# Dense experts of a diffusion step: first products of all chunks to DRAM, then the second products with three output tiles in PSUM

## The chip, the core and the metric

The kernel runs on one core of one Trainium2 chip. The metric is the device time of one launch in microseconds. Engines are named as the profile names them: PE (TensorE), DVE (VectorE), ACT (ScalarE), POOL (GpSimd), SP (SyncE, which only issues transfers here).

## The reference, cut to what matters

One layer of a diffusion backbone: modulated norm, attention and a linear recurrence, output projection, then a mixer of 16384 experts of which each token uses 16 for each of 8 heads. There are 256 context and 1024 latent tokens of 1024 features. The change is in the mixer:

```python
def peer(h, w_query, sub_keys, u_tab, v_tab):
    ...
        s1 = jnp.einsum('thq,hkq->thk', q1, sub_keys[:, 0]).astype(jnp.float32)
        s2 = jnp.einsum('thq,hkq->thk', q2, sub_keys[:, 1]).astype(jnp.float32)
        v1, i1 = lax.top_k(s1, PEER_TOPK)
        v2, i2 = lax.top_k(s2, PEER_TOPK)
        ...
        g = jax.nn.softmax(best, axis=-1)
        u = jnp.take(u_tab, eid, axis=0)
        act = jax.nn.gelu(jnp.einsum('td,thkd->thk', xb, u).astype(jnp.float32))
        vv = jnp.take(v_tab, eid, axis=0)
        return jnp.einsum('thk,thkd->td', (g * act).astype(vv.dtype), vv)
```

## The kernel before

Tokens stand in ten tiles of 128: two of context, eight latent. The mixer is computed in two ways side by side.

*Dense.* For six latent tiles (768 tokens) every expert is computed on PE, in 128 chunks of 128 experts (those that share a second key). `experts_in` (L692) makes a chunk's first products: it loads the chunk of the first table (`u`, 512 KB), splits it into two parts `uh` and `ul` that single-pass matmuls carry exactly (`split`, L132: ACT copies, another engine subtracts), and multiplies each of 8 slices of the features with the tokens' two parts `hh`, `hl`, in three matmuls (`mm3`, L137) for each of two blocks of 384 tokens: 48 matmuls of 128x384. The activations `a` are then multiplied with the routing weights `gt`, split into `ah`, `al`, and multiplied with the chunk's rows of the second table, `vh` and `vl`: six tiles, two halves of 512 features, three matmuls, so 36 matmuls of 128x512 (`dense`, L706). The results of two tiles stay in PSUM over all 128 chunks (`res`, four banks). For the other four, the products of a group of two chunks gather in a rotating bank (`rot`, two banks), which ACT copies out (`q`, L737) and DVE adds to `acc` in SBUF (L738). The first products of the first 34 chunks (`EARLY`) are taken beside the retrieval and go through DRAM (`ad`); for the others both products stand in one loop. Both splits subtract on POOL.

The weights `gt` come from DRAM too: `spread` (L644) makes, for each dense tile, one-hot matrices on DVE (`oh`), multiplies them on PE (`g`) and writes the weights of all experts to `gd`, twelve transfers of 4 MB.

*Gathered.* The two context tiles and the last two latent tiles fetch the rows of their experts: for each of 128 experts of a token one indirect transfer from POOL for each table (`mix`, L815), 512 KB into a row buffer, and one DVE operation (L829 for the first table, L843 for the second). There are 1024 of them. `tick` paces them: each piece of other work adds its estimated microseconds, and a row is issued for each `step` of them (L110). Four row buffers exist, and three more beside the dense loop (`N_MORE`).

*What sets the order.* A scheduler lays the program out once, by its own estimates, into one fixed list of instructions for each engine; an engine works through its list in order. So an instruction that waits holds up all behind it on its engine. Buffers of a pool are reused in turn, and a transfer into a buffer waits for its last reader.

The stages in the profile: modulations, context layer, latent projection, attention and norm up to 983 us; retrieval and spread of weights, with the first products of the first chunks between, to 1664 us; the dense loop with the gathered rows to the end.

## Time and profile before

| | before |
|---|---|
| median of 3 runs | 3830.61 us (3814.61 to 3831.82) |
| span of the profiled execution | 3810.7 us |
| PE busy | 3360.2 us, 88% |
| DVE busy | 3337.9 us, 88% |
| ACT busy | 1452.4 us, 38% |
| POOL busy | 2305.5 us, 61% |
| moved by DMA | 910.34 MB, 239 GB/s over the span |

The page gives the span of the profiled execution and no further time of it, so the span is compared with the runs. Two engines have the same share of the whole span, which says little: the stages differ, and a matmul's duration overlaps the next one's start. So the rows below are read by stretch, and for PE by the distance from one start to the next.

### The profile page before, as it was taken

What the parts mean: (1) busy time and instruction counts of PE and PEld (TensorE: products, weight loads), DVE (VectorE), ACT (ScalarE), POOL (GpSimd) and SP (SyncE); (2) the same over time, 40 slices, a digit from 0 to 9 for tenths busy, and PEclk for the clock granted to TensorE, in tenths of its full rate; (3) what the DMA queues carried; (4) which work ended last, traced back from release to release, by engine and by line L of the source; (5) the groups of instructions that cost most, each with busy time, mean ns of one, the idle gap of its engine ahead of it and who ended that gap; (6) DMA issues with size and microseconds to landing.
All of it is one profiled execution on the core that took longest, in us unless ns stands there. A gap on an engine that the chain in (4) does not pass through costs nothing.

```text
span 3810.7 us, 48687 instructions
## 1 busy us (share of the span) xinstructions
PE 3360.2 (88%) x16982; PEld 2714.7 (71%) x16982; DVE 3337.9 (88%) x6484; ACT 1452.4 (38%) x2270; POOL 2305.5 (61%) x1388
## 2 busy tenths in 40 slices
PE   7888869988798888878889999999999989999997
PEld 4476544433598877766667878888888878888786
DVE  4549886667889999958999999999999999999998
ACT  5634535543211345534333333333333333333333
POOL 0032664456611222136767888878888888888884
PEclk9799888999899999999999999999999999999998
DMA  8342654468810266778888888888888888888884
GB/s 331 119 148 81 216 208 140 146 214 292 278 45 23 79 193 197 209 244 305 299 298 282 287 299 288 305 294 300 298 292 292 298 302 298 292 297 296 293 302 175
DMA packets 344823, 910.34 MB, mean 239 GB/s; under 512 B 28664, under 2 KB 147064, under 8 KB 341504
## 3 DMA queue, kind: packets, MB, share of 16 engines
q0 software_dynamic: 147456, 536.94, 40.3%
q1 hardware_dynamic: 197120, 370.29, 29.3%
q8 instruction: 133, 2.18, 0.2%
q14 instruction: 114, 0.93, 0.1%
HBM read 830.55 MB, written 76.57 MB: 238 GB/s over the span
## 4 chain that ended last, share of the span: by engine, by line
DVE 29%; PE 23%; issue 10%; POOL 4%; DMA 2%; ACT 2%; SPq 0%; POOLq 0%; DVEq 0%; ACTq 0%
DVE acc L843 8%; PE u L138 5%; PE u L139 5%; PE u L140 5%; DVE row L829 4%; DVE acc L738 4%; DVE oh L676 2%; PE rot L138 2%; DVE oh L674 1%; DVE al L135 1%; DVE oh L677 1%; PE rot L140 1%; PE rot L139 1%; DVE oh L675 1%; POOL row L826 1%
## 5 line engine op out<-in xcount | busy, mean ns | idle before, releaser
L826 POOL DMA_INDIRECT row<-in_peer_u,eid x512 | 731.5, 1429 | 286.8 <-issue 81.1
L837 POOL DMA_INDIRECT row<-in_peer_v,eid x512 | 716.5, 1399 | 287.8 <-DVE acc L843 85.5
L843 DVE SCALAR_TENSOR_TENSOR acc<-row,w,acc 128x1024 f32<-128x1024 f32 x508 | 836.2, 1646 | 29.6 <-DMA row<-in_peer_v,eid 25.6
L829 DVE SCALAR_TENSOR_TENSOR row<-row,h 128x1024 f32<-128x1024 f32 x512 | 722.9, 1423 | 64.3 <-DMA row<-in_peer_u,eid 63.9
L138 PE MATMUL u<-hh,uh 128*128 128x384 f32 x2048 | 700.2, 342 | 12.7 <-ACT uh L134 9.5
L140 PE MATMUL u<-hh,ul 128*128 128x384 f32 x2048 | 698.8, 341 | 2.3 <-POOL ul L135 2.3
L139 PE MATMUL u<-hl,uh 128*128 128x384 f32 x2048 | 698.7, 341 | 0.0
L135 POOL TENSOR_TENSOR ul<-u,uh 128x1024 fp32r<-128x1024 f32 x128 | 335.4, 2635 | 369.9 <-ACT uh L134 353.9
L737 ACT ACTIVATE q<-rot 128x512 f32<-128x512 f32 x504 | 298.7, 596 | 675.6 <-DVE acc L738 373.0
L138 PE MATMUL rot<-vh,ah 128*128 128x512 f32 x1024 | 430.8, 421 | 115.7 <-ACT q L737 107.4
L738 DVE TENSOR_TENSOR acc<-q,acc 128x512 f32<-128x512 f32 x504 | 472.7, 943 | 36.2 <-ACT q L737 35.6
L139 PE MATMUL rot<-vl,ah 128*128 128x512 f32 x1024 | 411.5, 402 | 0.0
L140 PE MATMUL rot<-vh,al 128*128 128x512 f32 x1024 | 411.2, 402 | 0.0
L138 PEld LDWEIGHTS u<-hh,uh 128*128 128x128 f32 x2048 | 389.5, 190 | 18.1 <-ACT uh L134 10.4
L140 PEld LDWEIGHTS u<-hh,ul 128*128 128x128 f32 x2048 | 388.8, 190 | 3.7 <-POOL ul L135 2.7
L139 PEld LDWEIGHTS u<-hl,uh 128*128 128x128 f32 x2048 | 388.7, 190 | 2.2
L138 PEld LDWEIGHTS rot<-vh,ah 128*128 128x128 f32 x1024 | 199.5, 195 | 225.6 <-ACT q L737 188.3
L135 POOL TENSOR_TENSOR vl<-v,vh 128x1024 fp32r<-128x1024 f32 x128 | 330.5, 2584 | 27.9 <-ACT vh L134 25.9
L140 PE MATMUL mm<-hh,wl 128*128 128x256 f32 (+2 forms) x848 | 290.3, 343 | 7.4 <-POOL wl L135 5.7
L138 PE MATMUL mm<-hh,wh 128*128 128x256 f32 (+2 forms) x848 | 287.8, 339 | 5.0 <-ACT wh L134 5.0
L139 PE MATMUL mm<-hl,wh 128*128 128x256 f32 (+2 forms) x848 | 287.4, 339 | 0.0
L135 POOL TENSOR_TENSOR wl<-w,wh 128x1024 fp32r<-128x1024 f32 x46 | 113.4, 2467 | 242.4 <-ACT wh L134 242.3
(259 smaller groups left out, 6092.6 us busy)
## 6 DMA issues: line engine op xcount, KB each, us to landing
u<-in_ut SPq DMA_DIRECT2D x128, 512.0 KB, 4.3
v<-in_peer_v SPq DMA_DIRECT2D x128, 512.0 KB, 4.4
gd<-stg SPq DMA_DIRECT2D x12, 4096.0 KB, 16.4
gt<-gd SPq DMA_DIRECT2D x64, 768.0 KB, 7.6
w<-in_w_mod SPq DMA_DIRECT2D x24, 1024.0 KB, 7.6
w<-in_w_query SPq DMA_DIRECT2D x32, 512.0 KB, 3.7
w<-in_w_in SPq DMA_DIRECT2D x28, 512.0 KB, 5.0
ad<-a SPq DMA_DIRECT2D x68, 192.0 KB, 3.7
```

The lines of the kernel that those rows point to most:

```text
L135: return (eng or V).tensor_tensor(lo, src, hi, op=OP.subtract)
L138: T.matmul(out, lhs[0], rhs[0], start=first, stop=False)
L139: T.matmul(out, lhs[0], rhs[1], start=False, stop=False)
L140: T.matmul(out, lhs[1], rhs[0], start=False, stop=last)
L674: V.tensor_tensor(o1.rearrange(four, j=2), io, pairs(k1t, ts), op=OP.is_equal)
L676: V.tensor_tensor(oh.rearrange(four, j=2), o2.rearrange(four, j=2), pairs(gh, ts), op=OP.mult)
L737: A.activation(q, p, AF.Copy)
L738: tick(share / (2 * (N_DENSE - N_RES)), V.tensor_tensor(y, q, y, op=OP.add))
L826: G.indirect_dma_start(out=u, out_offset=None, in_=i["peer_u"], in_offset=bass.IndirectOffsetOnAxis(ap=eid[:, k:k + 1], axis=0))
L829: V.scalar_tensor_tensor(u, u, 1.0, h2, op0=OP.mult, op1=OP.mult, accum_out=act[:, j:j + 1])
L837: G.indirect_dma_start(out=v, out_offset=None, in_=i["peer_v"], in_offset=bass.IndirectOffsetOnAxis(ap=eid[:, k:k + 1], axis=0))
L843: V.scalar_tensor_tensor(acc, v, w[:, j:j + 1], acc, op0=OP.mult, op1=OP.add)
```

## The change

All 128 chunks' first products are computed first and written to DRAM (`ad`), beside the retrieval, the spread and a pass of their own (`phase("in")`); a second pass (`experts_out`, `phase("out")`) reads them back, chunk by chunk, with the second table and the weights. In the second pass PSUM holds three tiles (`N_RES`, six banks) and two rotating banks, in groups of four chunks; the buffers of the split tokens `hh`, `hl` are freed before it and serve the second table's splits, seven chunks deep. The subtraction of the second table's split is done by DVE, that of the first table's from chunk 60 on (`BESIDE`), and the 14 of the latent input projection. The first table's load buffer `u` is single in all first products (before: single for the early ones, double in the dense loop). The pacing constants of the gathered rows are new, and rows are now issued in the spread too.

```diff
-N_RES = 2
-GROUP = 2
-EARLY = 34
+N_RES = 3
+GROUP = 4
+AHEAD = 3
+BESIDE = 60
 F_STEP = 1.9
-D_STEP = 2.1
-STEP = {"spread": 1e9, "ret": 4.0}
-T_MUL = 2.0
-E_US = 3.0
-PE_US = 15.8
+STEP = {"spread": 3.3, "ret": 3.0, "in": 2.2, "out": 2.75}
+IN_US = 8.4
+OUT_US = 1.82
...
-            split(wh, wl, w, G if lat else V)
+            split(wh, wl, w)
...
-    ad = dram.tile([max(EARLY, 1), P, TD], F32, name="ad")
+    ad = dram.tile([P, P, TD], F32, name="ad")
...
-    def experts_in(raw, nraw, c, hh, hl, out):
-        u = raw.tile([P, KD, P], F32, name="u", bufs=nraw)
+    def experts_in(c, hh, hl):
+        u = eu.tile([P, KD, P], F32, name="u")
...
-        split(uh, ul, u, G)
+        if c < BESIDE:
+            split(uh, ul, u, G)
+        else:
+            tick(IN_US, split(uh, ul, u))
...
-            out(bs, p)
+            a = eu.tile([P, NB], F32, name="a", bufs=2)
+            A.activation(a, p, AF.Gelu_apprx_tanh)
+            nc.sync.dma_start(ad[c][:, bs], a)
...
+            NBUF = GROUP + AHEAD
+            def fetch(c):
+                v = wk.tile([P, D], F32, name="v", bufs=2)
+                nc.sync.dma_start(v, i["peer_v"].rearrange("(a b) d -> b a d", b=P)[c])
+                a = wk.tile([P, TD], F32, name="a", bufs=2)
+                nc.sync.dma_start(a, ad[c])
+                if c % 2 == 0:
+                    gts[0] = wk.tile([P, TD, 2], F32, name="gt", bufs=2)
+                    nc.sync.dma_start(gts[0], gd[c // 2])
+                vh = wk.tile([P, D], F32R, name="vh", bufs=NBUF)
+                vl = wk.tile([P, D], F32R, name="vl", bufs=NBUF)
+                tick(OUT_US, split(vh, vl, v))
+                tick(OUT_US, V.tensor_tensor(a, a, gts[0][:, :, c % 2], op=OP.mult))
+                ah = wk.tile([P, TD], F32R, name="ah", bufs=NBUF)
+                al = wk.tile([P, TD], F32R, name="al", bufs=NBUF)
+                tick(OUT_US, split(ah, al, a))
+                return c, ah, al, vh, vl
...
             for c0 in range(0, P, GROUP):
                 group = []
+                for c in range(c0, min(c0 + GROUP, P)):
+                    it = fetch(c)
+                    group.append(it)
                     if last:
-                        add(last)
+                        rotating(last)
                         last = None
+                    resident(it)
                 last = group
-            add(last)
+            rotating(last)
...
+        phase("in")
+        more.append(pool(ein, "gat2"))
+        for c in range(P):
+            experts_in(c, hha, hla)
+        more.clear()
+        behind.clear()
+    hs.close()
+    phase("out")
+    experts_out(dt)
```

How the lists of the engines change is shown at three places. In the changed kernel the lines behind the diff have moved: the gathered rows' DVE operations are L840 and L854 (L829 and L843 before), the add is L764 (L738), the multiplication with the weights L734 (L757), the gathers L837 and L848 (L826 and L837). `L135` is the subtraction of every split.

DVE in the middle of the dense loop, before:

```order
L135 TENSOR_TENSOR al<-a,ah 128x768
L843 SCALAR_TENSOR_TENSOR acc<-row,w,acc 128x1024
L757 TENSOR_TENSOR a<-a,gt 128x768
L829 SCALAR_TENSOR_TENSOR row,act<-row,h_16290 128x1024
L135 TENSOR_TENSOR al<-a,ah 128x768
L738 TENSOR_TENSOR acc_15477<-q,acc_15477 128x512
L829 SCALAR_TENSOR_TENSOR row,act<-row,h_16290 128x1024 x2
L738 TENSOR_TENSOR acc_15477<-q,acc_15477 128x512
L829 SCALAR_TENSOR_TENSOR row_21020,act<-row_21020,h_16290 128x1024
L738 TENSOR_TENSOR acc_15478<-q,acc_15478 128x512
```

DVE in the middle of the second pass, now:

```order
L764 TENSOR_TENSOR acc_22499<-q,acc_22499 128x512
L135 TENSOR_TENSOR al<-a,ah 128x768
L135 TENSOR_TENSOR vl<-v,vh 128x1024 x2
L764 TENSOR_TENSOR acc_22499<-q,acc_22499 128x512
L840 SCALAR_TENSOR_TENSOR row_27494,act<-row_27494,h_26479 128x1024
L135 TENSOR_TENSOR al<-a,ah 128x768
L844 TENSOR_TENSOR w<-w,gw_10139 128x16
L734 TENSOR_TENSOR a<-a,gt 128x768
L854 SCALAR_TENSOR_TENSOR acc<-row,w,acc 128x1024
L135 TENSOR_TENSOR vl<-v,vh 128x1024
L854 SCALAR_TENSOR_TENSOR acc<-row,w,acc 128x1024
L135 TENSOR_TENSOR al<-a,ah 128x768
```

The subtractions `vl` stand on DVE now, between fewer adds of `q`. (`h` holds the tokens of a gathered tile, `acc_` with a number a dense tile's sum, `acc` alone a gathered tile's.)

POOL in the middle of the dense loop, before:

```order
L837 DMA row_24001<-in_peer_v,eid_9835 128x1024
L135 TENSOR_TENSOR ul<-u,uh 128x1024 x2
L837 DMA row<-in_peer_v,eid_9835 128x1024 x3
L826 DMA row<-in_peer_u,eid_9835 128x1024
L826 DMA row_24047<-in_peer_u,eid_9835 128x1024
L826 DMA row_24060<-in_peer_u,eid_9835 128x1024
L826 DMA row_24129<-in_peer_u,eid_9835 128x1024
L135 TENSOR_TENSOR vl<-v,vh 128x1024
```

POOL in the middle of the second pass, now:

```order
L837 DMA row<-in_peer_u,eid_9887 128x1024
L848 DMA row<-in_peer_v,eid_9887 128x1024 x4
L848 DMA row_24788<-in_peer_v,eid_9887 128x1024
L848 DMA row<-in_peer_v,eid_9887 128x1024 x2
L848 DMA row_24898<-in_peer_v,eid_9887 128x1024
L848 DMA row_24930<-in_peer_v,eid_9887 128x1024
L848 DMA row_24937<-in_peer_v,eid_9887 128x1024
```

The subtractions `ul` and `vl` are gone from POOL, which only issues gathers there.

The end of DVE's list, before (`gt`, `v`: buffers that hold a dense tile's last norm):

```order
L809 SCALAR_TENSOR_TENSOR v<-v,rs_r,row 128x1024
L150 TENSOR_SCALAR rs_s<-rs_s 128x1
L145 TENSOR_SCALAR rs_m<-ss 128x1
L151 TENSOR_TENSOR rs_r<-rs_r,rs_s 128x1
L809 SCALAR_TENSOR_TENSOR gt<-gt,rs_r,row 128x1024
L149 TENSOR_SCALAR rs_s<-rs_r,rs_m 128x1
L150 TENSOR_SCALAR rs_s<-rs_s 128x1
L151 TENSOR_TENSOR rs_r<-rs_r,rs_s 128x1
L809 SCALAR_TENSOR_TENSOR gt<-gt,rs_r,row 128x1024
```

The end of DVE's list, now (`end`: the last dense tile's buffer; the rows are those of the last gathered tile):

```order
L820 SCALAR_TENSOR_TENSOR end_30878<-end_30878,rs_r,row 128x1024
L840 SCALAR_TENSOR_TENSOR row,act<-row,h_26479 128x1024 x5
L844 TENSOR_TENSOR w<-w,gw_10139 128x16
L854 SCALAR_TENSOR_TENSOR acc<-row,w,acc 128x1024 x16
L840 SCALAR_TENSOR_TENSOR row,act<-row,h_26479 128x1024 x16
L844 TENSOR_TENSOR w<-w,gw_10139 128x16
L854 SCALAR_TENSOR_TENSOR acc<-row,w,acc 128x1024 x16
L815 TENSOR_TENSOR acc<-acc,row 128x1024
L816 TENSOR_TENSOR row<-acc,row 128x1024
L145 TENSOR_SCALAR rs_m<-ss 128x1
```

Before, the list ends with the last norms of dense tiles; now 57 row operations of the last gathered tile stand behind the last add, 25 of L840 and 32 of L854.

By count, the new lists hold 330 row operations on DVE up to the last one-hot operation (222 before), 259 between that and the first multiplication with the weights, and 432 from there on. PE's list has 2084 first products up to the last product of the spread (1521 before), then 4060 more, then the 4608 second products. DVE's list holds 186 adds of `q` (504 before).

## Rows read from the trace of the kernel before

**Rows 1.** By stretch: start:end, us; busy (x count) of each engine; PE's clock, DMA share, GB/s.
```profile
0.00:983.00 983.00, 801.56 (x3253) 479.50 (x3253) 681.40 (x1584) 475.63 (x821) 405.54 (x285) 0.90 0.56 193
983.00:1312.00 329.00, 296.54 (x1815) 283.08 (x1816) 304.99 (x1890) 78.55 (x132) 86.58 (x46) 0.95 0.27 90
1312.00:1664.00 352.00, 313.48 (x2682) 273.33 (x2681) 343.47 (x957) 174.56 (x212) 74.71 (x24) 0.99 0.66 194
1664.00:1700.00 36.00, 21.59 (x119) 20.95 (x116) 1.25 (x1) 6.30 (x10) 7.57 (x5) 0.87 0.87 272
1700.00:2026.00 326.00, 273.44 (x1092) 210.95 (x1093) 309.95 (x331) 127.39 (x191) 224.44 (x131) 0.96 0.84 297
2026.00:3811.00 1785.00, 1653.59 (x8030) 1446.91 (x8028) 1696.84 (x1724) 589.99 (x907) 1506.66 (x898) 0.98 0.83 289
```
**Rows 2.** Groups of DVE, 1700 to 3811 us: busy us, mean ns, idle before.
```profile
L843 DVE SCALAR_TENSOR_TENSOR acc<-row,w,acc 128x1024 f32<-128x1024 f32 x399 | 686.5, 1720 | 3.8 <-DMA row<-in_peer_v,eid 1.0
L829 DVE SCALAR_TENSOR_TENSOR row<-row,h 128x1024 f32<-128x1024 f32 x400 | 585.3, 1475 | 15.2 <-DMA row<-in_peer_u,eid 15.2
...
L738 DVE TENSOR_TENSOR acc<-q,acc 128x512 f32<-128x512 f32 x504 | 472.7, 943 | 36.2 <-ACT q L737 35.6
...
L135 DVE TENSOR_TENSOR al<-a,ah 128x768 fp32r<-128x768 f32 x128 | 158.2, 1236 | 8.2 <-ACT ah L134 8.2
L757 DVE TENSOR_TENSOR a<-a,gt 128x768 f32<-128x768 f32 x127 | 142.7, 1123 | 27.8 <-ACT a L756 21.6 <-DMA a<-ad 4.2 <-issue 1.8
```
**Rows 3.** The same groups for the splits: POOL's two subtractions, ACT's copy.
```profile
L135 POOL TENSOR_TENSOR vl<-v,vh 128x1024 fp32r<-128x1024 f32 x127 | 328.1, 2586 | 17.0 <-ACT vh L134 15.0
...
L135 POOL TENSOR_TENSOR ul<-u,uh 128x1024 fp32r<-128x1024 f32 x94 | 235.6, 2526 | 1.0
...
L134 ACT ACTIVATE uh<-u 128x1024 fp32r<-128x1024 f32 x94 | 99.6, 1060 | 177.1 <-PE u L139 139.0 <-issue 31.8 <-PE u L140 3.8
```
**Rows 4.** Groups of DVE, 600 to 983 us, where POOL subtracts nothing.
```profile
L829 DVE SCALAR_TENSOR_TENSOR row<-row,h 128x1024 f32<-128x1024 f32 x75 | 90.9, 1221 | 28.7 <-DMA row<-in_peer_u,eid 28.3
L843 DVE SCALAR_TENSOR_TENSOR acc<-row,w,acc 128x1024 f32<-128x1024 f32 x64 | 82.9, 1295 | 14.6 <-DMA row<-in_peer_v,eid 13.9
...
L135 DVE TENSOR_TENSOR hl<-f,hh 128x1024 fp32r<-128x1024 f32 x7 | 8.5, 1219 | 0.0
```
**Rows 5.** Timeline of DVE, then of POOL, in the dense loop: start us, us.
```profile
2270.74 0.95 DVE L135 TENSOR_TENSOR al<-a,ah 128x768 fp32r<-128x768 f32 x1
...
2274.15 4.80 DVE L738 TENSOR_TENSOR acc<-q,acc 128x512 f32<-128x512 f32 x1 [1.32 <-ACT q L737]
2278.87 1.21 DVE L829 SCALAR_TENSOR_TENSOR row<-row,h 128x1024 f32<-128x1024 f32 x1
2280.01 0.08 DVE L829 DVE_READ_ACCUMULATOR row<-row,h 128x1 f32 x1
...
2281.16 0.68 DVE L738 TENSOR_TENSOR acc<-q,acc 128x512 f32<-128x512 f32 x1
...
2273.66 4.73 POOL L135 TENSOR_TENSOR ul<-u,uh 128x1024 fp32r<-128x1024 f32 x2
```
**Rows 6.** Timeline of PE in the dense loop: two second products, two first products.
```profile
2204.63 0.39 PE L138 MATMUL rot<-vh,ah 128*128 128x512 f32 x1
2204.86 0.39 PE L139 MATMUL rot<-vl,ah 128*128 128x512 f32 x1
...
2221.86 0.34 PE L140 MATMUL u<-hh,ul 128*128 128x384 f32 x1
2222.03 0.34 PE L138 MATMUL u<-hh,uh 128*128 128x384 f32 x1
```
**Rows 7.** DMA issues: engine, count, KB each, median us from issue to landing.
```profile
u<-in_ut SPq DMA_DIRECT2D x128, 512.0 KB, 4.3
...
gd<-stg SPq DMA_DIRECT2D x12, 4096.0 KB, 16.4
gt<-gd SPq DMA_DIRECT2D x64, 768.0 KB, 7.6
...
row<-in_peer_u,eid POOLq DMA_INDIRECT x512, 6.0
```
**Rows 8.** Longest wait, 1664 to 1740 us: us in total, times, longest.
```profile
DVE a L757 <- DMA v<-in_peer_v: 34.6, 1, 34.6
```

More of the change, by code (lines that the diff above doesn't have):

```diff
@@ L115, in tick @@
         ph = cur[0]
-        step = D_STEP if ph == "dense" else STEP.get(ph, F_STEP)
+        step = STEP.get(ph, F_STEP)
         while queue and clock[0] >= step:
@@ L129, in phase @@
         cur[0] = name
-        clock[0] = 0.0 if name == "dense" else clock[0]
+        clock[0] = 0.0 if name == "out" else clock[0]
     def split(hi, lo, src, eng=None):
@@ L718, in product, with resident, rotating @@
                 mm3(p, (ah[:, xs], al[:, xs]), (vh[:, cols], vl[:, cols]), c == first, c == last)
[L720 to L726 removed]
+            def resident(it):
+                for x in range(N_RES):
+                    for hf in range(2):
+                        product(res[x][hf], x, hf, it, 0, P - 1)
+            def rotating(group):
+                c0, c1 = group[0][0], group[-1][0]
                 for x in range(N_RES, N_DENSE):
@@ L737, in add @@
                             A.activation(q, p, AF.Copy)
[L738 removed]
+                            tick(OUT_US, V.tensor_tensor(y, q, y, op=OP.add))
             last = None
@@ L1000, in body @@
-    side[0] = "left"
-    phase("dense")
-    dense(dt, hha, hla)
+    with ExitStack() as ein:
+        eu = pool(ein, "eu")
+        eps = pool(ein, "eup", space=PSUM)
+        with ExitStack() as es:
+            vl = pool(es, "vl")
+            dense_picks.append(vl)
+            cb = pool(es, "cb")
+            with ExitStack() as e2:
+                found = choose(pool(e2, "sq"), pool(e2, "sqp", space=PSUM), [(dt, hha, hla), (gt[N_CTX:], hhb, hlb)], vl, cb)
+            hs2.close()
+            sp = pool(es, "lsp")
+            pp = pool(es, "lsq", 2, space=PSUM)
+            iota16.append(load("iota", [P, P], sp, F16))
+            phase("spread")
+            combine(cb, *found[dt[0]], dt[0], 1)
+            for x, t in enumerate(dt):
+                if x + 1 < N_DENSE:
+                    combine(cb, *found[t + 1], t + 1, 1)
+                spread(sp, pp, t, x)
+                tick(50)
+            phase("chB")
+            for t in gt[N_CTX:]:
+                combine(cb, *found[t], t, 1)
+            queue.extend(mix(t) for t in gt[N_CTX:])
+        phase("in")
[4 more added lines that the diff above has]
+        behind.clear()
```

79 lines of the change are left out of this document (12 added, 67 removed).

## The prediction

> **What bounds the kernel now.** I read the stretches first [rows 1]. From 2026 us on, 47% of the span, VectorE is busy 1696.84 of 1785 us (95%) and the DMA engines 0.83; the TensorE figure of 1653.59 overstates, since its matmuls overlap. Its real need comes from the pace of back-to-back starts. A first product (128x384) starts every 0.173 us and a second one (128x512) every 0.227 us [rows 6], so a chunk of experts is 48 x 0.173 = 8.3 us and 36 x 0.227 = 8.2 us, and the 94 full chunks there 1550 us, 87%. So VectorE is the bound of the dense loop, and TensorE is not far behind. From 983 to 1664 us (retrieval and spread, with 1521 first products) VectorE is busy 305 + 343 of 681 us, 95% too.
>
> Then I asked what fills VectorE. Gathered rows take 686.5 + 585.3 us, the adds of rotating sums 472.7, the splits and multiplications of activations 158.2 + 142.7 [rows 2]. These are long for their sizes. Before 983 us, where GpSimd splits nothing, a row takes 1.221 or 1.295 us and a 1024-wide subtraction 1.219 [rows 4], against 1.475 and 1.720 in the dense loop. The timeline shows why: an add that takes 0.68 us took 4.80 while GpSimd ran two splits of 4.73 together [rows 5]. All lengthenings after 1700 us: 399 x (1720 - 1295) + 400 x (1475 - 1221) + 504 x (943 - 680) + 128 x (1236 - 950) + 127 x (1123 - 950) ns = 462 us, with 127 + 94 splits on GpSimd [rows 3]. So one split there costs VectorE 2.09 us. Done by VectorE it costs 1.22.
>
> **Part by part.** *Splits.* 128 second-table splits and the 68 first-table splits from chunk 60 on go to VectorE: 196 x (2.09 - 1.22) = 171 us less. The Trainium skill (SBUF — State Buffer, "Who interferes with whom") says that a VectorE operation with two SBUF inputs and a GpSimd operation that reads SBUF hold each other off for a whole instruction; by it a split costs its full 2.5 us or so, and the saving would be some 250 us, an estimate. The 4.80 us agree in kind; the mean of 221 splits, 2.09, is what I use.
>
> *Adds.* Three tiles rotate instead of four, in groups of four chunks instead of two: 186 adds instead of 504, 318 x 0.68 = 216 us less on VectorE, and the same off ScalarE's evictions, which have room.
>
> *The 14 splits of the latent input projection* go to VectorE too; TensorE sets that stage, so I cost them at nothing. Were they all exposed they would cost 14 x 1.22 = 17 us; were GpSimd's hold all on the path, they would gain 12.
>
> So VectorE loses 387 us in all. That isn't the gain, because the change also splits the work into stages with different limits. Each is summed with counts from the new order.
>
> *Up to 983 us:* unchanged.
>
> *Retrieval and spread (681 us, VectorE-bound).* 108 more gathered rows are handled before the last one-hot operation (330 against 222), as the spread may now gather too. A row's mean of 1.26 us, less about 0.07 by which it overlaps its successor (2278.87 to 2280.01 in [rows 5]), gives 108 x 1.19 = 129 us. About a dozen more first-table splits on GpSimd (43 chunks done here against 31) add some 15 us, and a piece of a combine moves out, some -10. In [rows 7] a write of weights to DRAM lands 16.4 us after its issue, and before no row was gathered beside those twelve. If every one delays a row in front of VectorE by half its time, that is 100 us, if none, nothing; the rows come on another queue, so I take 5 us. Sum 820 us. TensorE's 563 more matmuls here, 98 us, fit into its idle time.
>
> *Rest of the first products.* 4060 matmuls x 0.1733 = 704 us, at the granted 0.98 clock [rows 1] 718 us. VectorE has only some 475 us here: 259 rows, 68 splits and what GpSimd's last splits hold. The first table's buffer is now single, so a chunk's loop is load 4.3 us [rows 7], ScalarE 1.06 and GpSimd 2.53 [rows 3] with a gather of up to 1.5 ahead: 9.4 us against 8.3 for the 17 chunks still split by GpSimd, 18 us at most. With VectorE it is 4.3 + 1.06 + 1.22 + a row of 1.30 = 7.9 us, under 8.3. I take 732 us.
>
> *Second pass.* TensorE: 4608 x 0.2267 = 1045 us, by the clock 1066. Start: the activations and weights come back from DRAM only after the buffers of the first products are free; the weights land in 7.6 us [rows 7], then a multiplication, two splits: 14 us. VectorE until the last add: of 432 rows all but 57, 186 adds, 256 activation operations of 0.95 [rows 5] and 128 splits: 479 + 127 + 243 + 156 + 15 us = 1020 us, 936 to 1020 with the overlaps. DMA: 375 rows and 128 chunks of the second table at 0.524 MB, activations 50 MB, weights 50 MB: 364 MB, against 289 GB/s at a share of 0.83 [rows 1], so 348 at a full share and 1047 us. Three engines between 1020 and 1066 us will not fit into each other without waits; VectorE alone reached 95% with the others at 83 and 87%. I add 40 us. Below that, nothing; above, see the first rival.
>
> *Tail.* In VectorE's new order 57 rows stand after the last add; before, none did. They use four buffers again: a landing of 6.0 us [rows 7] and a row's 1.3, by four, 1.83 us each: 104 us, and 8 us for the last norm. Nothing covers this.
>
> *A gap that goes.* At 1664 to 1700 us VectorE waited 34.6 us for the dense loop's first weights and rows [rows 8]. It is replaced by the 14 us above.
>
> Sum: 983 + 820 + 732 + 14 + 1066 + 40 + 112 = 3767 us of span, against 3810.7. No own time of the profiled execution is shown; the median run, 3830.61, is 20 us above its span, the fastest 4. Against the median I forecast 3787 us, 1.1% less. About 0.5% is what a measurement of this kernel can tell from no change.
>
> On the DMA term, the HBM Reference of the Trainium skill ("Specifications") gives some 425 GB/s for a core that streams alone. The second pass would then need 857 us of transfers, an estimate, and the 40 us could fall away; no run here shows that rate, and the sum goes by 348.
>
> **Rivals.** (1) *The transfers set the second pass: slower.* It must move 364 MB in 1120 us, 325 GB/s, while the dense loop sustains 289. If the DMA engines can hold no more than that with seven rows in flight, the pass takes 364 / 0.289 = 1261 us and the time is 3928 us. It decides from 1164 us, 313 GB/s, on. For it: VectorE's rows wait in order, so a late row stops the splits that TensorE needs. Against: VectorE set the 289, not the DMA engines, which were idle 17%. Chance 0.21.
>
> (2) *The single buffer sets the first products: slower.* If that load lands like a gathered row, in 6.0 us, the loop is 9.6 us and 68 chunks cost 1.3 us more each: 88 us, 3875 us. Against: 4.3 us was measured with the DMA engines as busy as here. Chance 0.10.
>
> (3) *Each stage runs at its longest engine:* retrieval 800, first products 718, second pass 14 + 1066, tail 104: 3685 of span, 3705 us. For it: VectorE is off the bound in both passes, which takes the waits of matmuls for evictions with it. Chance 0.18.
>
> (4) *GpSimd is not what lengthens VectorE's operations,* so they stay at their long durations [rows 2]: the second pass's VectorE work is then 223 x 1.72 + 209 x 1.55 + 186 x 0.94 + 128 x (1.24 + 1.12 + 1.65) us and small things, 1430 us in all, some 1320 before the tail: 983 + 820 + 732 + 1320 + 112 + 20 = 3987 us. The Trainium skill (Perfetto Trace Analysis, "Optimizing Scalar/DVE Operations") advises handing work of a saturated VectorE to GpSimd, which speaks against this change, and warns of the shared port in the same place. The rows alone and the timeline [rows 4, 5] leave little of it: chance 0.04.
>
> **How the numbers follow.** My forecast, 3745 to 3830 us, has 0.47. Nine tenths of its lower and middle part and all of (3) are faster by over 0.5% (under 3811): 0.56. Its upper end and the mild forms of (1) and (2) are within 0.5%: 0.18. The rest of (1), (2) and (4) is slower: 0.26. The range, 3690 to 3890 us, leaves out the harsh half of (1), (4) and a little of (3).
>
> **What would show it.** A row of 1.22 to 1.30 us and an add of 0.68 us in the second pass: the step on GpSimd is right. Matmuls starting every 0.173 us over the first products, without gaps before a chunk: the single buffer is harmless. A DMA share over 0.9 with VectorE waiting for rows: (1). A stretch of some 110 us at the end with TensorE idle: the tail. Wrong I would be above all if the second pass, without the tail, takes over 1160 us, or if retrieval grows by much more than 139 us because rows land late beside the weights' writes.

## The result, and the profile after

The changed kernel takes 3879.03 us (median of four runs, 3864.99 to 3900.28), the kernel before 3831.22: a ratio of 1.014, 95% interval 1.010 to 1.018. I forecast 3787 us. The sign was wrong.

The profiled execution has a span of 3886.5 us. Its stretches, cut where the steps of the prediction are cut: up to the first product, to the first one-hot product of the spread, to its last, to the last first product, to the last sum of rotating tiles, to the end (columns as in [rows 1]: start:end, length, busy time and count of PE, PEld, DVE, ACT and POOL, PE's clock, DMA share, GB/s):

```profile
0.00:955.00 955.00, 801.28 (x3254) 480.56 (x3255) 660.78 (x1574) 471.36 (x817) 350.10 (x258) 0.91 0.56 190
955.00:1333.00 378.00, 333.87 (x1997) 319.14 (x1995) 358.41 (x2003) 92.19 (x152) 146.68 (x94) 0.94 0.46 150
1333.00:1808.00 475.00, 395.23 (x3071) 353.88 (x3071) 429.04 (x917) 184.37 (x228) 210.32 (x112) 0.95 0.79 252
1808.00:2546.00 738.00, 714.96 (x4058) 707.83 (x4057) 419.12 (x606) 169.24 (x270) 373.00 (x276) 0.99 0.85 299
2546.00:3744.00 1198.00, 1090.75 (x4611) 885.26 (x4609) 943.84 (x1153) 342.16 (x467) 527.28 (x375) 0.96 0.86 310
3744.00:3887.00 143.00, 0.00 (x0) 0.00 (x0) 95.27 (x129) 9.86 (x19) 76.30 (x63) 0.50 0.72 242
```

| step | predicted, us | measured, us |
|---|---|---|
| up to the first product | 983 | 955 |
| retrieval and spread | 820 | 853 |
| rest of the first products | 732 | 739 |
| second pass, with its start, to the last sum | 14 + 1066 + 40 = 1120 | 1197 |
| tail | 112 | 143 |
| span | 3767 | 3887 |
| median less span | +20 | -7 |

Against [rows 1], VectorE is no longer the bound anywhere behind the spread: it is busy 57% of the first products and 79% of the second pass. TensorE should have taken over, but by my sum it needs only 1066 of the second pass's 1198 us, and behind 3744 us it stands still.

VectorE's operations did shrink as forecast. DVE, 2546 to 3744 us (busy us, mean ns | idle before), answering [rows 2, 4]:

```profile
L854 DVE SCALAR_TENSOR_TENSOR acc<-row,w,acc 128x1024 f32<-128x1024 f32 x191 | 244.1, 1278 | 0.0
L840 DVE SCALAR_TENSOR_TENSOR row<-row,h 128x1024 f32<-128x1024 f32 x185 | 224.4, 1219 | 111.3 <-DMA row<-in_peer_u,eid 111.3
L135 DVE TENSOR_TENSOR vl<-v,vh 128x1024 fp32r<-128x1024 f32 x128 | 155.5, 1218 | 36.4 <-ACT vh L134 36.3
L764 DVE TENSOR_TENSOR acc<-q,acc 128x512 f32<-128x512 f32 x186 | 126.0, 684 | 15.5 <-ACT q L763 15.4
L135 DVE TENSOR_TENSOR al<-a,ah 128x768 fp32r<-128x768 f32 x128 | 122.0, 953 | 20.4 <-ACT ah L134 20.2
L734 DVE TENSOR_TENSOR a<-a,gt 128x768 f32<-128x768 f32 x128 | 121.7, 953 | 77.2 <-DMA a<-ad 67.5 <-DMA gt<-gd 4.4 <-issue 3.8
```

A row takes 1219 or 1278 ns where it took 1475 or 1720, a sum 684 where it took 943. New is the idle time: 111 us in front of rows that have not landed.

Landings, 2030 us to the end (KB each, median us from issue to landing), answering [rows 7]:

```profile
v<-in_peer_v SPq DMA_DIRECT2D x128, 512.0 KB, 6.4
a<-ad SPq DMA_DIRECT2D x128, 384.0 KB, 6.4
...
u<-in_ut SPq DMA_DIRECT2D x58, 512.0 KB, 6.2
...
row<-in_peer_u,eid POOLq DMA_INDIRECT x320, 6.6
```

The same for `v` in the dense loop of before (2030 to 3810 us):

```profile
v<-in_peer_v SPq DMA_DIRECT2D x95, 512.0 KB, 4.4
```

What the engines wait for in 1000 us of the second pass, 2600 to 3600 (us in total, times, longest):

```profile
ACT vh L134 <- DMA v<-in_peer_v: 278.2, 54, 12.6
...
ACT ah L134 <- DVE a L734: 168.3, 49, 9.4
...
DVE row L840 <- DMA row<-in_peer_u,eid: 98.0, 40, 7.6
PEld rot L138 <- ACT q L763: 95.2, 34, 8.2
```

The last line is most of the loss; the clock of 0.96 goes with it. Its cause reads in the timeline of the second pass (start us, us, operation, in brackets the idle time and its releaser), where TensorE waits 6.27 us:

```profile
2944.09 0.33 SPq L725 DMA_DIRECT2D v<-in_peer_v  x1
...
2950.84 1.06 ACT L134 ACTIVATE vh<-v 128x1024 fp32r<-128x1024 f32 x1 [5.06 <-DMA v<-in_peer_v]
2951.80 0.83 ACT L134 ACTIVATE ah<-a 128x768 fp32r<-128x768 f32 x1
...
2953.93 0.95 DVE L734 TENSOR_TENSOR a<-a,gt 128x768 f32<-128x768 f32 x1
...
2954.92 0.84 ACT L134 ACTIVATE ah<-a 128x768 fp32r<-128x768 f32 x1 [2.29 <-DVE a L734]
2955.67 1.06 ACT L763 ACTIVATE q<-rot 128x512 f32<-128x512 f32 x2
...
2956.30 0.79 PE L138 MATMUL rot<-vh,ah 128*128 128x512 f32 x1 [6.27 <-ACT q L763]
```

ScalarE works its list in order. The evictions `q`, for which the two rotating banks wait, stand behind copies of a later chunk: `vh` waits for a load issued 6.75 us earlier, then `ah` for VectorE. TensorE is held up by parts that it needs only later.

### The profile page after: what moved, and what is told of

The parts are those of the page before. It is cut to its first block, busy times and chain, and to the rows that moved or that the text cites. A ratio compares the mean times of both kernels' runs of the same rounds, so it can differ in the third digit from the quotient of the medians.

```text
span 3886.5 us, 48466 instructions
## 1 busy us (share of the span) xinstructions
PE 3336.1 (86%) x16982; PEld 2746.7 (71%) x16982; DVE 2906.5 (75%) x6377; ACT 1269.2 (33%) x1952; POOL 1683.7 (43%) x1177
## 4 chain that ended last, share of the span: by engine, by line
DMA 25%; DVE 21%; PE 16%; issue 15%; POOL 8%; ACT 3%; POOLq 0%; ACTq 0%; DVEq 0%; SPq 0%
DMA u<-in_ut 8%; DMA row<-in_peer_u,eid 5%; POOL row L837 4%; DMA ad<-a 4%; POOL row L848 3%; DMA row<-in_peer_v,eid 3%; DVE acc L854 2%; DMA v<-in_peer_v 2%; DVE row L840 2%; PE po L460 2%; DMA a<-ad 2%; PE u L138 2%; PE u L140 2%; PE u L139 2%; DVE ul L135 2%
## 5 line engine op out<-in xcount | busy, mean ns | idle before, releaser
L848 POOL DMA_INDIRECT row<-in_peer_v,eid x512 | 686.2, 1340 | 806.1 <-DVE acc L854 342.5
L837 POOL DMA_INDIRECT row<-in_peer_u,eid x512 | 685.3, 1338 | 701.5 <-DVE row L840 301.0
L840 DVE SCALAR_TENSOR_TENSOR row<-row,h 128x1024 f32<-128x1024 f32 x512 | 637.5, 1264 | 178.6 <-DMA row<-in_peer_u,eid 178.2
L854 DVE SCALAR_TENSOR_TENSOR acc<-row,w,acc 128x1024 f32<-128x1024 f32 x508 | 662.1, 1303 | 50.5 <-DMA row<-in_peer_v,eid 45.9
L138 PE MATMUL rot<-vh,ah 128*128 128x512 f32 x768 | 314.8, 410 | 86.3 <-ACT q L763 85.6
L138 PE MATMUL res<-vh,ah 128*128 128x512 f32 x768 | 301.4, 392 | 12.7 <-ACT ah L134 12.7
L139 PE MATMUL rot<-vl,ah 128*128 128x512 f32 x768 | 309.6, 403 | 0.0
L140 PE MATMUL rot<-vh,al 128*128 128x512 f32 x768 | 309.0, 402 | 0.0
L140 PE MATMUL res<-vh,al 128*128 128x512 f32 x768 | 300.2, 392 | 4.1 <-DVE rs_m L145 2.3
L135 DVE TENSOR_TENSOR ul<-u,uh 128x1024 fp32r<-128x1024 f32 x68 | 83.3, 1225 | 292.8 <-ACT uh L134 292.8
L139 PE MATMUL res<-vl,ah 128*128 128x512 f32 x768 | 301.3, 392 | 0.0
L134 ACT ACTIVATE uh<-u 128x1024 fp32r<-128x1024 f32 x128 | 135.6, 1060 | 479.4 <-DMA u<-in_ut 390.5
L135 POOL TENSOR_TENSOR ul<-u,uh 128x1024 fp32r<-128x1024 f32 x60 | 161.5, 2691 | 252.6 <-ACT uh L134 247.9
```

Source lines behind the costliest of these rows:

```text
L134: A.activation(hi, src, AF.Copy)
L135: return (eng or V).tensor_tensor(lo, src, hi, op=OP.subtract)
L138: T.matmul(out, lhs[0], rhs[0], start=first, stop=False)
L139: T.matmul(out, lhs[0], rhs[1], start=False, stop=False)
L140: T.matmul(out, lhs[1], rhs[0], start=False, stop=last)
L837: G.indirect_dma_start(out=u, out_offset=None, in_=i["peer_u"], in_offset=bass.IndirectOffsetOnAxis(ap=eid[:, k:k + 1], axis=0))
```

## Experiments

"Pass" is the time from the first multiplication by the weights to the last sum (1189 us in the changed kernel), "end" what follows it (143 us), "first products" from the last product of the spread to the last first product (739 us). Ratios are to the kernel before on the same chip.

| run | median, us | ratio, 95% interval | first products | pass | end |
|---|---|---|---|---|---|
| changed kernel | 3879 | 1.0138 (1.0096 to 1.0179) | 739 | 1189 | 143 |
| a2_norows | 3648 | 0.9515 (0.9495 to 0.9536) | 757 | 1065 | 11 |
| c1_touch | 3884 | 1.0149 (1.0085 to 1.0214) | 749 | 1213 | 123 |
| c2_nofetch | 3703 | 0.9671 (0.9631 to 0.9712) | 739 | 1051 | 104 |
| a1_vbuf | 3870 | 1.009 (1.0071 to 1.0109) | 741 | 1178 | 142 |
| c3_rows10 | 3822 | 0.997 (0.9947 to 0.9993) | 734 | 1139 | 133 |
| e1_rows_v | 3764 | 0.9828 (0.9805 to 0.985) | 732 | 1078 | 135 |
| d4_tail7 | 3859 | 1.0082 (1.0048 to 1.0117) | 738 | 1203 | 114 |
| a3_early | 3793 | 0.9903 (0.9886 to 0.9919) | 816 | 1152 | 12 |
| d3_early_u2 | 3746 | 0.9803 (0.9768 to 0.9838) | 786 | 1150 | 12 |
| d2_even | 3707 | 0.9708 (0.9668 to 0.9748) | 746 | 1137 | 12 |
| e2_even_v | 3647 | 0.9523 (0.9489 to 0.9557) | 748 | 1077 | 12 |
| d1_vgps | 4029 | 1.053 (1.0492 to 1.0567) | 739 | 1336 | 142 |
| b1_vsplit (from before) | 3764 | 0.982 (0.9803 to 0.9836) | | | |
| b2_vloop (from before) | 3640 | 0.9502 (0.947 to 0.9533) | | | |

### What the gathered rows cost the second pass: their work, or their coming

Without rows in the second pass and behind it:

```diff
+                if cur[0] in ("out", "tail"):
+                    continue
                 u = row()
...
+                if cur[0] in ("out", "tail"):
+                    continue
                 v = row()
```

> The changed kernel without the gathered rows of the second pass and of the stretch behind it: about 488 rows are neither fetched nor multiplied, all else stands. Both W and L expect a second pass of 1070 to 1100 us (4608 matmuls at 0.2267 us and a clock of 0.97 are 1077) and an end of 25 to 40 us instead of 143. Theory E (the evictions of the rotating banks cost TensorE time by themselves, whatever else runs): the pass stays above 1160 us. Total 3665 to 3690 by W and L, above 3750 by E.

The pass fell to 1065 us and the end to 11, a little below what W and L asked for (the theories of a1_vbuf, further down: late loads that block ScalarE's list, and the transfers as such). Theory E is dead: two rotating banks and ScalarE's evictions cost nothing by themselves. The rows cost 124 us of the pass and 132 of the end. Next, the two halves of a row apart. Rows fetched, but not worked on:

```diff
+                    if cur[0] in ("out", "tail"):
+                        V.tensor_copy(act[:, j:j + 1], u[:, 0:1])
+                    else:
                         V.scalar_tensor_tensor(u, u, 1.0, h2, op0=OP.mult, op1=OP.mult, accum_out=act[:, j:j + 1])
...
+                    if cur[0] in ("out", "tail"):
+                        V.tensor_copy(acc[:, k:k + 1], v[:, 0:1])
-                    if k == 0:
+                    elif k == 0:
```

> The changed kernel, in which VectorE only touches one column of each gathered row of the second pass and of the end: rows are fetched and waited for in the same places, but the 1.2 to 1.3 us of work on each is left out. In the changed kernel the second pass (first multiplication by the weights to the last sum) takes 1189 us, without rows 1065. Theory B (the rows cost TensorE time because VectorE is busy with them when a chunk's parts are due): the pass falls to 1070 to 1095. Theory R (VectorE waits in its list for late rows, and what TensorE needs stands behind) and theory L (the transfers of the rows delay those of the chunks): it stays at 1150 to 1190. Total about 3740 by B, 3800 to 3850 by R and L.

Rows worked on, but not fetched:

```diff
+                far = cur[0] in ("out", "tail")
+                if not far:
                     G.indirect_dma_start(out=u, out_offset=None, in_=i["peer_u"],
...
-                    V.scalar_tensor_tensor(u, u, 1.0, h2, op0=OP.mult, op1=OP.mult, accum_out=act[:, j:j + 1])
+                    V.scalar_tensor_tensor(u, h2 if far else u, 1.0, h2, op0=OP.mult, op1=OP.mult, accum_out=act[:, j:j + 1])
...
+                far = cur[0] in ("out", "tail")
+                if far:
+                    v = h2
+                else:
                     G.indirect_dma_start(out=v, out_offset=None, in_=i["peer_v"],
```

> The opposite of the run before: in the second pass and at the end VectorE does the full work of every row, on data that lie in SBUF, and the rows are not fetched. Theory B: the pass stays at 1150 to 1190 us. Theories R and L: 1065 to 1095, and the end shrinks from 143 us to some 85 (57 rows at 1.3 us and the norms). Total about 3840 by B, 3710 by R and L.

The same 1000 us of c1_touch, and three of its waits:

```profile
2600.00:3600.00 1000.00, 913.16 (x3866) 743.23 (x3865) 456.38 (x816) 284.55 (x389) 366.72 (x318) 0.96 0.84 309
```
```profile
ACT vh L134 <- DMA v<-in_peer_v: 201.7, 52, 11.8
...
DVE act L842 <- DMA row<-in_peer_u,eid: 194.3, 62, 7.6
...
DVE acc L856 <- DMA row<-in_peer_v,eid: 150.4, 64, 6.0
```

And of c2_nofetch:

```profile
2600.00:3600.00 1000.00, 995.65 (x4393) 824.11 (x4391) 886.82 (x1101) 321.90 (x437) 3.88 (x2) 1.00 0.47 158
```

In c1_touch VectorE is busy 46% and TensorE gets no more done than in the changed kernel (3866 matmuls in the 1000 us, 3869 there). In c2_nofetch VectorE is busy 89% and TensorE runs without a gap. So less work for VectorE buys nothing in this pass; most of its freed time turns into waiting for rows (194 and 150 us, against 98 in the changed kernel). Theory B is dead; both totals, 3884 and 3703, lie by R and L, the first 34 us above their range, the second 7 below. What costs is the coming of the rows: that they come late, or the bytes that they bring. ScalarE's wait for `v` costs nothing by itself: in c2_nofetch it is still 201 us.

### Late rows, late loads, or the rate

```diff
-AHEAD = 3
+AHEAD = 2
...
-                v = wk.tile([P, D], F32, name="v", bufs=2)
+                v = wk.tile([P, D], F32, name="v", bufs=4)
...
-                a = wk.tile([P, TD], F32, name="a", bufs=2)
+                a = wk.tile([P, TD], F32, name="a", bufs=3)
```

> The changed kernel with four buffers for the loads v of the second pass instead of two and three for a instead of two (their split parts keep six buffers instead of seven, to make room). Theory W: ScalarE works its list in order, its copies vh wait 317 us for late loads of v, and behind them stand the evictions q that TensorE's two rotating banks wait for. Then the wait of vh for v falls below 100 us, the waits of TensorE for q go with it, and the second pass takes 1130 to 1160 us instead of 1198: total about 3830. Theory L (the transfers as such set the pass): the loads only queue earlier, the pass stays at 1185 to 1210 and the total at 3865 to 3895.

ScalarE's wait for `v` fell from 278 us to nothing, and yet the pass by 11 us only; the total is theory L's. The same stretch, its waits:

```profile
ACT ah L134 <- DVE a L734: 354.3, 30, 21.0
...
DVE row L840 <- DMA row<-in_peer_u,eid: 91.6, 29, 6.3
```

The wait moved: from `vh` to `ah`, which VectorE makes, and VectorE still waits for rows. Theory W had the blocked list right and its cause half right. Then the rows alone:

```diff
-AHEAD = 3
-N_MORE = 3
+AHEAD = 2
+N_MORE = 6
```

> The changed kernel with ten gathered rows in flight beside the dense work instead of seven (the split parts keep six buffers instead of seven, to make room). Theory R: a row is issued some 4 us earlier, VectorE's wait for rows falls from 104 us to under 40, and the pass from 1189 us to 1130 to 1150: total about 3835. Theory L and theory B: the pass stays at 1175 to 1200, total 3860 to 3890.

The pass took 1139 us, as theory R has it, and VectorE's wait for rows of `peer_u` fell from 98 to 18 us. ScalarE's wait for `v` stayed:

```profile
ACT vh L134 <- DMA v<-in_peer_v: 271.0, 54, 9.8
```

So a part of the cure; is the rest that wait, or is it the rate of the transfers (329 GB/s at a share of 0.90 here)? Both edits at once, `AHEAD` now 1:

```diff
-AHEAD = 3
-N_MORE = 3
+AHEAD = 1
+N_MORE = 6
...
-                v = wk.tile([P, D], F32, name="v", bufs=2)
+                v = wk.tile([P, D], F32, name="v", bufs=4)
...
-                a = wk.tile([P, TD], F32, name="a", bufs=2)
+                a = wk.tile([P, TD], F32, name="a", bufs=3)
```

> The changed kernel with ten rows in flight, four buffers for v and three for a (the split parts keep five buffers instead of seven, to make room). Ten rows alone took the second pass from 1189 us to 1139, four buffers for v alone to 1178, and without any rows it is 1065. If the rest, 74 us, is ScalarE's list waiting for late v while rows no longer hold up VectorE, both together give 1085 to 1105 and a total of 3775 to 3790. If the rest is the transfers' own rate (share 0.90 at 328 GB/s with ten rows), or the parts' five buffers are too few, the pass stays at 1130 to 1145 and the total at 3810 to 3830.

1078 us, better than the first reading asked for. The same 1000 us:

```profile
2600.00:3600.00 1000.00, 987.09 (x4322) 811.50 (x4321) 886.54 (x1098) 311.88 (x432) 536.96 (x357) 1.00 0.93 348
```

and two of its groups there (idle before | what ended it):

```profile
L138 PE MATMUL rot<-vh,ah 128*128 128x512 f32 x720 | 280.4, 389 | 2.8 <-ACT q L763 2.8
...
L134 ACT ACTIVATE vh<-v 128x1024 fp32r<-128x1024 f32 x119 | 122.2, 1052 | 0.0
```

Alone the edits gave 11 and 50 us, together 111 of the 124. I read them as one loop: a late row delays VectorE, which frees the buffers of `v` and `a` late; their loads come late, ScalarE stalls, and VectorE is late again. Either end left short keeps the loop. That the edits work together is shown; the loop is argued from the waits. The rate was no limit: the transfers ran at 348 GB/s once there was somewhere to put them. Whether `v` or `a` needed its buffers was not separated.

On the mean the buffers of the changed kernel suffice: 376 rows in 1189 us use up seven buffers in 22 us, and 128 chunks two of `v` in 19 us, against landings of 6 to 8 us. The waits for rows come at places: in the pass VectorE waits before `peer_u` rows alone, for `peer_v` not at all. At one such place GpSimd issues a row of `peer_v`, then one of `peer_u`; VectorE's list takes the later one first and waits for it, while the older, landed at 2809.76, is used behind it:

```profile
2802.08 1.42 POOL L848 DMA_INDIRECT row<-in_peer_v,eid  x1 [0.64 <-DVE acc L854]
2804.14 1.42 POOL L837 DMA_INDIRECT row<-in_peer_u,eid  x1 [0.64 <-DVE acc L854]
...
2812.47 1.22 DVE L840 SCALAR_TENSOR_TENSOR row<-row,h 128x1024 f32<-128x1024 f32 x1 [2.06 <-DMA row<-in_peer_u,eid]
...
2816.44 1.28 DVE L854 SCALAR_TENSOR_TENSOR acc<-row,w,acc 128x1024 f32<-128x1024 f32 x1
```

Whether another order of the rows would have done as much as more buffers was not tried.

### The tail

```diff
             rotating(last)
+            behind.clear()
+            tick(1e9)
             more.clear()
```

> The changed kernel with only its end altered: the 57 gathered rows behind the last sum come before the last norms of the dense tiles, while all seven buffers are still there, instead of after them with four. If the end is set by a row's landing over the number of buffers (57 x 6.9 / 4 = 98 us, and 40 for the norms), it becomes 57 x 1.28 = 73, VectorE's own pace, and 20 to 30 for the norms: 95 to 105 us instead of 143, total 3835 to 3845. If the order or VectorE sets it, it stays at 130 to 150.

The end took 114 us instead of 143, 9 above the range; eight of the 57 rows now came ahead of the last sum, and the total, 3859, is 14 above its range, as the pass did not get shorter. The two halves of a row tell more. With rows that take VectorE hardly any time the end lasts 123 us (c1_touch), with rows worked on but not fetched 104 (c2_nofetch; 85 were expected), with both 143. So VectorE's own work, rows and norms, is the larger part, and the landings over four buffers add some 39 us. In the changed kernel VectorE's rows behind 3744 us (busy us, mean ns | idle before) were

```profile
L854 DVE SCALAR_TENSOR_TENSOR acc<-row,w,acc 128x1024 f32<-128x1024 f32 x32 | 41.2, 1287 | 18.0 <-DMA row<-in_peer_v,eid 17.6
...
L840 DVE SCALAR_TENSOR_TENSOR row<-row,h 128x1024 f32<-128x1024 f32 x25 | 30.6, 1225 | 16.7 <-DMA row<-in_peer_u,eid 16.4
```

106 us with the waits; the rest is the dense tiles' last norms, which stand ahead of most of these rows, and the gathered tile's own norm. But no way of running 57 rows there is as good as having none:

### Rows moved into the first products

```diff
-BESIDE = 60
+BESIDE = 44
...
-STEP = {"spread": 3.3, "ret": 3.0, "in": 2.2, "out": 2.75}
+STEP = {"spread": 3.3, "ret": 3.0, "in": 1.68, "out": 2.75}
```

> The changed kernel with more gathered rows in the first products, where VectorE is busy 57%: its first-table splits come to VectorE from chunk 44 instead of 60, and a row is placed per 1.68 us of other work instead of 2.2. 420 rows instead of 259 stand there, 271 instead of 432 behind, none after the last sum. Theory P (the rows stand in the wrong stage: 135 us without rows from 1808 to 1943, and 57 rows behind the last sum): the end shrinks from 143 to 40 us, the second pass from 1198 to 1130, the first products grow by at most 20 from 739: total about 3730. Rival C: the single buffer of the first table takes over, since five rows a chunk delay its load and its split; the first products then grow by 80 us or more and the total is 3790 or above.

The end shrank to 12 us, the pass by 37 to 1152. But the first products took 816 us, 77 more, and the total is 3793, about what rival C asks for. The DMA engines were full (1950 to 2550 us):

```profile
1950.00:2550.00 600.00, 551.63 (x3062) 532.80 (x3061) 467.98 (x560) 123.93 (x204) 409.16 (x321) 0.99 1.00 382
```

Is it the single buffer of the first table, or that share of 1.00? With a second buffer from chunk 44 on:

```diff
-        u = eu.tile([P, KD, P], F32, name="u")
+        u = (eu if c < 44 or c % 2 else eu2[0]).tile([P, KD, P], F32, name="u")
...
         more.append(pool(ein, "gat2"))
+        eu2.append(pool(ein, "eu2"))
```

> The run with 420 rows in the first products again, with a second buffer for the first table from chunk 44 on. In that run the first products took 816 us instead of 739, the DMA engines were busy all the time (share 1.00, 380 GB/s), and ScalarE waited 504 us for loads of the first table. If the single buffer is what lengthens them, they fall to 740 to 765 us and the total to 3725 to 3745. If the transfers have reached their limit, the second buffer gives nothing: 800 to 820 us, total 3780 to 3800.

786 us, between the two. Transfers went from 382 to 396 GB/s at a share that was full already (1950 to 2500 us):

```profile
1950.00:2500.00 550.00, 520.50 (x2913) 514.08 (x2912) 447.53 (x539) 118.41 (x192) 403.65 (x304) 0.98 1.01 396
```

Both count: 30 us are the buffer's, and the other 47 over the changed kernel's 739 I put down to too many bytes in one stage, by that share. So the rows want spreading evenly, 336 and 355:

```diff
-BESIDE = 60
-AHEAD = 3
-N_MORE = 3
+BESIDE = 44
+AHEAD = 2
+N_MORE = 6
...
-STEP = {"spread": 3.3, "ret": 3.0, "in": 2.2, "out": 2.75}
+STEP = {"spread": 3.3, "ret": 3.0, "in": 2.1, "out": 2.75}
```

> The changed kernel with the rows spread evenly (336 in the first products, 355 behind, none after the last sum; first-table splits on VectorE from chunk 44) and ten rows in flight beside the dense work. If late rows in VectorE's list, too few of them in the first products and the 57 behind the last sum are all that the change lost, the first products take 740 to 755 us, the second pass 1085 to 1120 and the end 15 to 40: total 3655 to 3720. If the transfers as such set a floor, both passes run at no more than the 310 to 330 GB/s of the changed kernel's second pass, the second pass stays at 1130 to 1150 and the total at 3740 to 3780.

First products 746 us, as expected, and the end 12, below the 15 to 40; but the pass 1137, as in c3_rows10 and above the 1085 to 1120, with ScalarE's wait for `v` as long (270 us). With the buffers of e1_rows_v added (`AHEAD` 1, four for `v`, three for `a`):

> The same buffers with the rows spread evenly (336 in the first products, 355 behind): without the v buffers 3707 us, with a second pass of 1137. By the first reading above 1080 to 1100 and a total of 3655 to 3670, still above the 3640 of the kernel before with its loop's splits on VectorE; by the second 3700 to 3715.

3647 us, with a pass of 1077. 4.8% under the kernel before: the reading that asked for 3655 to 3670 holds, and the time is 8 below its range.

### The splits

One part undone, the second pass's splits back on GpSimd:

```diff
-                tick(OUT_US, split(vh, vl, v))
+                tick(OUT_US, split(vh, vl, v, G))
```

> The changed kernel with one part undone: the 128 splits vl of the second pass back on GpSimd. By my price (2.09 us of VectorE for a split on GpSimd, 1.22 for one on VectorE) VectorE has 111 us more of lengthened operations there and reaches 88%; if late rows set the pass (theory R), GpSimd's own time counts too, since the gathers are issued behind splits of 2.5 us: 60 to 120 us longer, total 3940 to 4000. Rival: VectorE and GpSimd both have room in the pass, so that nothing changes: 3865 to 3890.

150 us longer than the changed kernel, 147 of it in the pass, and beyond the 60 to 120 expected. DVE from 2555 to 3891 us:

```profile
L854 DVE SCALAR_TENSOR_TENSOR acc<-row,w,acc 128x1024 f32<-128x1024 f32 x191 | 305.3, 1599 | 1.9 <-DMA row<-in_peer_v,eid 1.1
L840 DVE SCALAR_TENSOR_TENSOR row<-row,h 128x1024 f32<-128x1024 f32 x185 | 278.7, 1514 | 129.3 <-DMA row<-in_peer_u,eid 124.6 <-issue 4.3
L135 DVE TENSOR_TENSOR al<-a,ah 128x768 fp32r<-128x768 f32 x128 | 165.8, 1298 | 12.5 <-ACT ah L134 12.2
L734 DVE TENSOR_TENSOR a<-a,gt 128x768 f32<-128x768 f32 x128 | 164.3, 1284 | 124.3 <-DMA a<-ad 101.8 <-DMA gt<-gd 20.3 <-issue 2.3
L764 DVE TENSOR_TENSOR acc<-q,acc 128x512 f32<-128x512 f32 x186 | 156.8, 850 | 38.6 <-ACT q L763 38.6
```

The lengthenings are 191 x 0.321 + 185 x 0.295 + 128 x 0.345 + 128 x 0.331 + 186 x 0.166 = 233 us, 1.82 us for each of 128 splits, against the 2.09 that I took. The Trainium skill says that handing work of a saturated VectorE to GpSimd may make sense, and warns that the two share a port, so that it might not help (Perfetto Trace Analysis, "Optimizing Scalar/DVE Operations"). The trace bears out the warning: the 128 splits took 156 us off VectorE and lengthened its other operations by 233.

That is 77 us net; where the rest of the 147 arose was not separated. VectorE's idle time before rows grew by 20 us (131 for 111), before the multiplication with the weights by 47 (124 for 77) and before the sums by 23 (39 for 16), so rows that land late behind GpSimd's splits are by themselves a small part. That less work bought nothing in c1_touch does not say what more work costs.

And one part alone, in the kernel before:

```diff
-        split(uh, ul, u, G)
+        split(uh, ul, u)
...
-                    split(vh, vl, v, G)
+                    split(vh, vl, v)
```

> The kernel before with one part of the change alone: the splits ul and vl of its dense loop on VectorE instead of GpSimd, nothing else. By my price (2.09 us that a split on GpSimd costs VectorE, 1.22 on VectorE itself, 221 splits) 192 us less: about 3640. Rows fall to 1.22 and 1.30 us, adds to 0.68. Rival: VectorE's relief is met by the transfers; the loop moves its bytes at no more than the 310 GB/s of the second pass instead of 290, so that 2110 us become 1970: about 3690. Rival S: VectorE's work does not shrink (the long durations have another cause) and the 256 splits add 1.22 us each: about 4100.

Only 66 us less, by none of the expectations. The stretches of the spread and of the dense loop:

```profile
1312.00:1664.00 352.00, 264.80 (x2125) 221.94 (x2124) 321.71 (x981) 152.92 (x179) 0.00 (x0) 0.73 0.57 163
...
2026.00:3600.00 1574.00, 1552.31 (x7703) 1385.47 (x7702) 1457.88 (x1870) 584.76 (x885) 997.58 (x697) 1.00 0.90 325
```

The loop is what I promised, and more: TensorE is busy 1552 of 1574 us, it is the bound now. The loss lies ahead of it. Beside the retrieval VectorE is the bound, so a first-table split there waits in its list while GpSimd idles; 1590 + 2125 matmuls ran from 983 to 1664 us, where [rows 1] has 1815 + 2682, and the loop's first second product came at 1840 us instead of about 1700. At the end of the spread 15 chunks had their first products, against 31 before (the expectation below has 19). So with the splits taken ahead left where they were:

```diff
-        split(uh, ul, u, G)
+        split(uh, ul, u, G if c < EARLY else V)
...
-                    split(vh, vl, v, G)
+                    split(vh, vl, v)
```

> The kernel before with the splits of its dense loop on VectorE, but those of the 34 first products taken ahead left on GpSimd, which is free beside the retrieval. With all of them on VectorE the loop ran at 134 us per 8 chunks, TensorE's own pace, but the loop began 140 us late, as only 19 first products instead of 31 were done by the end of the spread. With this edit 12 x 8.3 = 100 us of that come back: total 3650 to 3670, 1664 us and 97 first and 128 second products of 8.4 and 8.25 us each behind it being 3535 as a floor. If the first part is not what was lost, it stays at 3740 to 3770.

3640 us, 187 less than before, 5.0%, and 10 below the range: with 15 chunks in place of 19, 16 x 8.3 = 133 us were to come back, and 124 did. The same two stretches:

```profile
1312.00:1664.00 352.00, 310.27 (x2612) 271.32 (x2611) 342.73 (x1025) 170.92 (x210) 72.76 (x23) 0.98 0.64 190
...
2026.00:3600.00 1574.00, 1558.83 (x7830) 1408.39 (x7829) 1439.41 (x1832) 573.38 (x868) 972.49 (x692) 1.00 0.89 322
```

222 splits moved at a price difference of 0.87 us are 193 us, by the price of the prediction. VectorE's own figures bear it out: behind 1700 us a row takes 1.22 or 1.28 us and a sum 0.69, all of [rows 2] is 465 us shorter, and the 222 splits take 270, so 195 us net. That the time fell by nearly the same is partly luck, since TensorE now sets the loop. This kernel and e2_even_v are the fastest here, 3640 and 3647 us, within each other's spread, and both run TensorE almost without gaps through their last part.

## Why the prediction was wrong, point by point

**Splits on GpSimd lengthen VectorE's operations: right,** in mechanism and size (2.09 us taken, 1.82 in d1_vgps; 193 us by the sum for 222 splits, 195 in b2_vloop). The fourth rival is dead.

**VectorE loses 387 us of work: about right, and the wrong thing to count.** Its busy time fell by 431 us, from 3337.9 to 2906.5. But the splits alone bring the old loop to TensorE's pace (b2_vloop, with all 504 sums), so the 216 us of sums had nothing left to give; and c1_touch took another 400 us of work off VectorE without moving the pass.

**Second pass, 40 us of waits and a clock of 0.98: the step that failed.** I compared three engines' sums, 1020 to 1066 us, and added a small number for friction. The measured loss is 117 us over the 14 and 1066: waits for `q`, and a clock of 0.96 that goes with them, since it is 1.00 wherever the waits are gone. What I left out is time to land against buffers: a load takes 6.4 us and has two buffers, a row 6.6 and seven, and both stand in in-order lists whose later entries TensorE needs at once. On the mean these buffers suffice, so that a mean would not have shown it either; by the order in which the lists take what lands, they did not. With more of both, the pass fell to 1078 us (e1_rows_v). I used the 7.6 us of [rows 7] for the start only. My argument for the first rival, a late row that stops VectorE's list, was the mechanism; I put it under a rate. Its point of decision, 313 GB/s, was beside the matter: the pass ran at 310 with the DMA engines 14% idle, and e1_rows_v at 348.

**Tail, 112 us: mechanism right, size wrong.** The 57 rows on four buffers came and took 106 us with their waits, for 104 in the sum; but they came behind the dense tiles' norms, which I took to be hidden, and 143 us in all. That it need not exist I did not weigh: VectorE had 43% of the first products free, and no row was placed between 1808 and 1943 us.

**First products, 732 us: right (739), by luck.** `u` did not land in 4.3 us, as I took it, but in 6.2, as the second rival feared; and the row of 1.3 us that I put into the loop hardly stood in it. The chunks that VectorE splits followed each other at 8.67 us: 6.23 to land, 1.06 and 1.23 for the split, 0.16 between (medians). That is just over TensorE's 8.3, so the single buffer sets the pace and costs little. ScalarE waits for it (1808 to 2546 us):

```profile
ACT uh L134 <- DMA u<-in_ut: 357.2, 65, 9.4
```

At 420 rows `u` lands in 6.7 us, a chunk takes 9.4, and it costs a lot.

**Up to the first product, unchanged: 28 us off, in my favour.** All kernels with the 14 latent splits on VectorE start their first products at 934 to 971 us, the three without at 983 to 990. I allowed 12. The last attention score is already 23 us earlier (780 for 803). That it is these splits is likely, but VectorE also works on 13 fewer rows ahead of that point (189 for 202); neither was tried alone.

**Retrieval, 820 us: 33 short.** VectorE's busy time grew by the 139 us of the sum, from 648 to 787, but partly by chance: beside GpSimd's splits a row took 1.47 us there, not 1.26. The 33 are idle time, 65 us instead of 33: one-hots waited 39 us for the products of earlier ones (7 before), rows 25 us for their landing (10 before). The shift at the first product nearly cancels them.

**Third rival, each stage at its longest engine, 3705 us:** not what happened, but e1_rows_v and e2_even_v show that its picture of the passes can be had, with buffers.

**From span to median I added 20 us;** it was -7. The difference between the one profiled execution and the median is noise of that size and carries no term.

## What to carry to other kernels

Before counting what an engine saves, ask what the stage will be bound by afterwards, and compare for each transfer its landing time under load with the time that its buffers cover, by the order in which the lists take what lands and not on the mean alone; where loads end in in-order lists, short buffers at two places hold each other up, and mending one shows little. Splitting one mixed loop into stages also splits its transfers and its filler work, which must then be spread over the stages anew. And take the smallest part of a change alone first: here moving the dense loop's splits to VectorE was worth 5%, and the restructuring around it, as made, cost it all and more.

## What the runs showed of the hardware

- How long a load takes to land cannot be told from the share of the DMA engines: `v` landed in 4.8 us at a share of 0.48 (a2_norows), in 4.8 at 0.79 (d1_vgps), in 4.4 at 0.83 (before) and in 6.4 at 0.86 (the changed kernel). What sets it stays open.
- A share of 1.00 is not one rate: 382 GB/s with one buffer for the first table (a3_early), 396 with two (d3_early_u2). The Trainium skill (HBM Reference, "Specifications") has some 425 GB/s for a core that streams alone; no run here reached it.
- TensorE's clock, as the mean of a stretch, went with its waits: 1.00 of full speed (2.4 GHz) where there were no gaps (c2_nofetch, e1_rows_v), 0.96 with 95 us of waits for `q` in 1000 (the changed kernel), 0.92 with 161 (d1_vgps), and 0.73 in the spread of b1_vsplit, where TensorE had the fewest first products to fill its waits for one-hots. The time that this costs is part of what the waits cost: in e1_rows_v it came back with them.
